# The MLP's up projection by one level of Strassen's recursion, in two passes of 1024 latent tokens, with the context tokens apart in native fp32

## The chip, the cores and the metric

The kernel runs on one core of one Trainium2 chip, in one launch. The metric is the device time in microseconds (us) of that core. The engines are TensorE (PE; its weight loads are listed as PEld), VectorE (DVE), ScalarE (ACT), GpSimd (POOL) and SyncE (SP), which issues most of the DMAs. All data is fp32; an fp32 number goes through TensorE either as native fp32 or, rounded, as fp32r.

## The reference, cut to what matters

One layer of a hybrid DeltaNet / Conformer backbone with a gated MLP, for 2048 latent tokens (a grid of 32 rows of 64) and 128 context tokens of width 1024. The change touches the first half of the MLP alone:

```python
h = rmsnorm(x, g_pre_ffn) * (1.0 + scale_f) + shift_f
gt, up = jnp.split(h @ w_up, 2, axis=-1)          # w_up: 1024 x 5632
gt = (dwconv2d_grid(gt, conv_ffn) if grid else dwconv1d(gt, conv_ffn[1])) + b_conv_ffn
y = (jax.nn.silu(gt) * up) @ w_down               # w_down: 2816 x 1024
x = x + gate_f * rmsnorm(y, g_post_ffn)
```

The depthwise convolution is 3x3 over the grid for latent tokens and 3 taps along the row for context tokens. `h` and `w_up` are split by both kernels into a high fp32r part and a low rest; a product is then three fp32r matmuls: high by high, high by low, low by high.

## The kernel before, in words

The stages follow each other: norm and input projection, short convolutions and the gated delta rule, output projection (lines up to 1173), MLP up (1177 to 1308), MLP down (1311 to 1366). Features lie on the partitions, tokens along the row. A scheduler orders each engine's instructions; every engine runs its own list in order and waits on semaphores.

The output projection handles 17 chunks of 128 tokens: the context chunk first, chunks 8 to 15, and chunks 0 to 7 last. After the matmuls of a chunk (line 1122), its norm runs on ACT and DVE (1131 to 1145), TensorE transposes it (1151) and ACT writes the normed, modulated chunk `ht` (1154). Chunks 0 to 7 are split at once into `h2H` and `h2L` in SBUF (1158, 1159); the others go to the DRAM tensor `d_h2` and are read back and split at lines 1207 to 1210.

MLP up has 44 weight tiles of 128 columns: 22 for the gate half, 22 for the up half. `load_up` (1190) brings one tile from DRAM, ACT writes its high part (1196), POOL the low rest (1197). `project_up` (1212) multiplies the tile with all 2176 tokens in blocks of 512, 512, 512, 320 and 320, each with 8 slices of the contraction times 3 matmuls (1220 to 1222). For a gate tile, `gate_in` copies the result into the padded grid `gb` on ACT (1245); `gate_conv` runs the 9 taps on DVE over all 2048 latent tokens (1256, then 8 times 1258), the context row beside it (1260, 1262), and silu on ACT (1263). For an up tile, `do_up` multiplies the PSUM block into `acc` on DVE (1269) and sends `acc` to the DRAM tensor `d_y`. The convolution of tile j runs beside the matmuls of up tile j-1 and of gate tile j+1.

MLP down reads `d_y` back by token chunk, splits it (1335 on ACT, 1336 on DVE), and multiplies with 22 weight tiles `wd`, each split by ACT (1323) and DVE (1324), in two halves of 512 output columns, 2244 matmuls in all (1339 to 1341). The weights of the first half are loaded and split while MLP up still runs.

## Time and profile before

| what | value |
|---|---|
| median of 3 runs | 2883.85 us (2879.0 to 2900.59) |
| span of the profiled execution, first to last instruction | 2883.5 us |
| MLP up on TensorE, first matmul to the first one of MLP down | 1309.07 to 2360.50, 1051.4 us |
| MLP down on TensorE, first matmul to the end of the span | 2360.50 to 2883.5, 523 us |
| DVE busy in the span | 1760.5 us, 61% |
| POOL busy in the span | 574.1 us, 20% |

The profiled execution is the span; nothing else is known to lie around it, and it agrees with the median to 0.4 us. The profile lists groups of instructions by source line with busy time, mean duration and the idle time before them; the timeline lists instructions with start and duration. A duration reaches from the start of an instruction to its end, and back-to-back instructions of one engine overlap a little, so the spacing of starts is what an instruction costs its engine.

### The profile page before, as it was taken

To read this page: it belongs to the slowest core of one execution; us is meant where nothing else is said; L and a number is where in the kernel's file an instruction comes from. 1 tells how busy PE (TensorE), PEld (TensorE's weight loads), DVE (VectorE), ACT (ScalarE), POOL (GpSimd) and SP (SyncE) were. 2 spreads that over 40 slices of the span, in tenths; PEclk is the share of its full clock that TensorE was granted. 3 is DMA by queue.
4 is the path that set the end of the run, shared out by engine and by line. 5 is a ranking of instruction groups with operands and counts; after the bars stand their busy time and mean duration, and the time that the engine had idled before them with its cause. 6 is when DMAs were issued, how large, how long until landed. Compare 5 with 4: busy or idle time off the path is not lost.

```text
span 2883.5 us, 40010 instructions
## 1 busy us (share of the span) xinstructions
PE 2769.5 (96%) x16077; PEld 2362.1 (82%) x16077; DVE 1760.5 (61%) x1929; ACT 962.6 (33%) x1992; POOL 574.1 (20%) x629
## 2 busy tenths in 40 slices
PE   7999999788899999999999999999999999999998
PEld 4888888677788887887888888888888888888887
DVE  4898999976667755564967454555555463224443
ACT  6432222445666656663111111111111122224221
POOL 2210011267165643222311111111111100000000
PEclk9999999899889999999999999999999999999999
DMA  7033522565886636643122111111111153336543
GB/s 266 20 90 115 149 83 70 113 188 132 228 261 182 188 111 242 195 137 125 49 72 83 38 54 38 54 38 53 38 54 38 50 169 111 98 97 203 173 164 119
DMA packets 341365, 337.77 MB, mean 117 GB/s; under 512 B 113990, under 2 KB 258620, under 8 KB 340924
## 3 DMA queue, kind: packets, MB, share of 16 engines
q1 hardware_dynamic: 329372, 321.59, 37.2%
q10 hardware_dynamic: 11808, 13.63, 1.4%
q8 instruction: 126, 2.06, 0.3%
q14 instruction: 59, 0.48, 0.1%
HBM read 240.35 MB, written 94.81 MB: 116 GB/s over the span
## 4 chain that ended last, share of the span: by engine, by line
PE 65%; DMA 5%; DVE 3%; POOL 3%; SPq 2%; ACT 2%; issue 2%; DVEq 0%; ACTq 0%; POOLq 0%
PE ps L1222 12%; PE ps L1220 12%; PE ps L1221 12%; PE ps L1122 6%; PE ps L1339 6%; PE ps L1341 6%; PE ps L1340 6%; SPq L164 1%; DMA ws<-in_wdown_dram 1%; DVE dm L817 1%; POOL bigB L150 1%; POOL prod L147 1%; PE p L955 1%; PE p L943 1%; PE p L925 1%
## 5 line engine op out<-in xcount | busy, mean ns | idle before, releaser
L1220 PE MATMUL ps<-h2H,wr 128*128 128x512 f32 (+1 forms) x1760 | 634.2, 360 | 3.1 <-DVE wr L1196 3.1
L1222 PE MATMUL ps<-h2H,wr 128*128 128x512 f32 (+1 forms) x1760 | 633.0, 360 | 1.7 <-POOL wr L1197 1.7
L1221 PE MATMUL ps<-h2L,wr 128*128 128x512 f32 (+1 forms) x1760 | 633.5, 360 | 0.0
L1258 DVE SCALAR_TENSOR_TENSOR acc<-gb,pvf,acc 128x2048 f32<-128x2048 f32 x176 | 419.5, 2388 | 1.3
L1220 PEld LDWEIGHTS ps<-h2H,wr 128*128 128x128 f32 x1760 | 330.7, 188 | 49.8 <-DVE wr L1196 3.4
L1222 PEld LDWEIGHTS ps<-h2H,wr 128*128 128x128 f32 x1760 | 330.8, 188 | 48.8 <-POOL wr L1197 2.1
L1221 PEld LDWEIGHTS ps<-h2L,wr 128*128 128x128 f32 x1760 | 330.8, 188 | 46.2
L359 PE MATMUL ps<-hH,wr 128*128 128x512 f32 (+1 forms) x960 | 349.7, 369 | 6.4 <-ACT bigA L410 4.1
L360 PE MATMUL ps<-hL,wr 128*128 128x512 f32 (+1 forms) x960 | 352.3, 367 | 0.0
L361 PE MATMUL ps<-hH,wr 128*128 128x512 f32 (+1 forms) x960 | 349.6, 365 | 0.0
L1197 POOL TENSOR_TENSOR wr<-wt,wr 128x1024 fp32r<-128x1024 f32 x44 | 128.9, 2930 | 882.7 <-ACT wr L1196 879.3
L1339 PE MATMUL ps<-wd,yr 128*128 128x512 f32 x748 | 291.9, 391 | 2.7 <-ACT wd L1323 2.6
L1340 PE MATMUL ps<-wd,yr 128*128 128x512 f32 x748 | 291.7, 390 | 0.0
L1341 PE MATMUL ps<-wd,yr 128*128 128x512 f32 x748 | 291.2, 390 | 0.0
L1256 DVE TENSOR_SCALAR acc<-gb,pvf 128x2048 f32<-128x2048 f32 x22 | 29.6, 1346 | 411.2 <-ACT gb L1245 405.7
L373 DVE SCALAR_TENSOR_TENSOR acc<-bigA,pvt,acc 128x1024 f32<-128x1024 f32 (+2 forms) x168 | 250.5, 1491 | 11.7 <-ACT acc L370 7.5
L359 PEld LDWEIGHTS ps<-hH,wr 128*128 128x128 f32 x960 | 183.8, 193 | 33.0 <-ACT bigA L410 4.6
L361 PEld LDWEIGHTS ps<-hH,wr 128*128 128x128 f32 x960 | 185.2, 193 | 25.1 <-issue 2.6
L360 PEld LDWEIGHTS ps<-hL,wr 128*128 128x128 f32 x960 | 185.5, 193 | 23.9 <-issue 1.6
L1336 DVE TENSOR_TENSOR yr<-yt,yr 128x1408 fp32r<-128x1408 f32 x68 | 110.6, 1626 | 150.5 <-ACT yr L1335 150.5
L1196 ACT CAST wr<-wt 128x1024 fp32r<-128x1024 f32 x43 | 45.4, 1056 | 446.0 <-issue 423.7
L1245 ACT COPY gb<-ps 128x512 f32<-128x512 f32 (+2 forms) x110 | 55.2, 503 | 362.2 <-PE ps L1222 349.9
...
## 6 DMA issues: line engine op xcount, KB each, us to landing
...
```

The costliest lines, as they stand in the source:

```text
L359: nc.tensor.matmul(ps[:, 0:n], wr[:, 0, k], hH[bi][:, k], start=(k == 0), stop=False)
L360: nc.tensor.matmul(ps[:, 0:n], wr[:, 0, k], hL[bi][:, k], start=False, stop=False)
L361: nc.tensor.matmul(ps[:, 0:n], wr[:, 1, k], hH[bi][:, k], start=False, stop=(k == KD - 1))
L373: nc.vector.scalar_tensor_tensor(dst, src[:, o + t:o + t + n], w[:, t:t + 1], dst, ALU.mult, ALU.add)
L1122: nc.tensor.matmul(pss[hf][:], a[:, k], w[k][:, 512 * hf:512 * hf + 512], start=(w is woH and a is mH and k == KD - 1), stop=(w is woL and ...
L1220: nc.tensor.matmul(ps[:, 0:n], wr[:, 0, k], h2H[bi][:, k], start=(k == 0), stop=False)
L1221: nc.tensor.matmul(ps[:, 0:n], wr[:, 0, k], h2L[bi][:, k], start=False, stop=False)
L1222: nc.tensor.matmul(ps[:, 0:n], wr[:, 1, k], h2H[bi][:, k], start=False, stop=(k == KD - 1))
L1258: nc.vector.scalar_tensor_tensor(al, gb[:, t // 3:t // 3 + 32, t % 3:t % 3 + 64], w[:, t:t + 1], al, ALU.mult, ALU.add)
L1339: nc.tensor.matmul(ps[:], yr[:, 0, i], wd[:, 0], start=(q == 0 and i == 0), stop=False)
L1340: nc.tensor.matmul(ps[:], yr[:, 0, i], wd[:, 1], start=False, stop=False)
L1341: nc.tensor.matmul(ps[:], yr[:, 1, i], wd[:, 0], start=False, stop=(q == 1 and i == HN - 1))
```

## The change

MLP up is rewritten. The context chunk is taken out: `ctx_unit` multiplies its 128 tokens with unsplit fp32 weights, 16 native fp32 matmuls of 128 columns for each of 22 units. The latent tokens are done in two passes p of 1024 tokens. In a pass the 1024 x 1024 block of `h` is cut in quarters (two halves of the contraction by two halves of the tokens), and a pair of weight tiles (gate tile j, up tile j) likewise. Strassen's recursion in Winograd's form makes 7 products of the 8: `build_T` forms the 7 token operands T0 to T6 once in a pass, `prep` the 7 weight operands for each unit (p, j), and `product` is 4 slices times 3 matmuls of 512 columns. So a unit has 84 matmuls of 512 columns; there are 44 units. `unit` adds the products up: in PSUM where two share a bank, else on DVE and POOL. `gate` runs the convolution for the 15 (p = 0) or 17 (p = 1) grid rows that a pass can finish; two rows and a strip of `up` go through the new DRAM tensor `d_hal` to the second pass.

All chunks of the output projection now go to `d_h2`; the SBUF copies of chunks 0 to 7 are gone. The first tap moves from DVE to ACT. The scheduler's order of every engine is unchanged up to the end of the output projection.

```diff
-            if c < 8:
-                o = slice(c % 4 * P, c % 4 * P + P)
-                nc.vector.tensor_copy(h2H[c // 4][:, :, o], ht[:])
-                nc.vector.tensor_tensor(h2L[c // 4][:, :, o], ht[:], h2H[c // 4][:, :, o].bitcast(F32), ALU.subtract)
-            else:
-                nc.scalar.dma_start(d_h2[:, :, c * P:(c + 1) * P], ht[:])
+            nc.scalar.dma_start(d_h2[:, :, c * P:(c + 1) * P], ht[:])
...
-        def project_up(m):
-            nonlocal npb
-            wr = first.pop() if first else load_up(m)
-            for bi in range(5):
-                s, n = BLOCKS[bi]
-                ps = (pmm if npb % 8 else pmx).tile([P, 512], F32, name="ps4", tag="mm")
-                npb += 1
-                for k in range(KD):
-                    nc.tensor.matmul(ps[:, 0:n], wr[:, 0, k], h2H[bi][:, k], start=(k == 0), stop=False)
-                    nc.tensor.matmul(ps[:, 0:n], wr[:, 0, k], h2L[bi][:, k], start=False, stop=False)
-                    nc.tensor.matmul(ps[:, 0:n], wr[:, 1, k], h2H[bi][:, k], start=False, stop=(k == KD - 1))
-                yield s, n, ps
...
+        hc = gp.tile([P, KD, P], F32, name="hc")
+        nc.sync.dma_start(hc[:], d_h2[:, :, CTX * P:NTOK])
...
+        T = [tp.tile([P, 2, HK, 512], F32R, name=f"T{i}") for i in range(7)]
...
+        def raw(src):
+            t = rp.tile([P, HK, P], F32, name="raw", tag="raw")
+            nc.sync.dma_start(t[:], src)
+            return t
+
+        def quarters(j):
+            return [raw(wup[m, :, HK * q:HK * q + HK, :]) for m in (j, NF + j) for q in range(2)]
...
+        def ctx_unit(j):
+            qs = quarters(j)
+            gpr = gprs[j % 2]
+            ps = pmm.tile([P, 2, P], F32, name="psc", tag="mm")
+            for g in range(2):
+                for k in range(KD):
+                    nc.tensor.matmul(ps[:, g], qs[2 * g + k // HK][:, k % HK], hc[:, k], start=(k == 0), stop=(k == KD - 1))
+            nc.scalar.copy(gpr[:, 1:129], ps[:, 0])
...
+        def split(dst, src, eng):
+            nc.scalar.copy(dst[0], src)
+            eng.tensor_tensor(dst[1], src, dst[0].bitcast(F32), ALU.subtract)
+
+        def build_T(p, k):
+            f = lambda t: t[:].rearrange("p a b -> p (a b)")
+            o = 1024 * p
+            b11, b21, b12, b22 = (raw(d_h2[:, kk, a:a + 512].rearrange("p (a b) -> p a b", b=P))
+                                  for a in (o, o + 512) for kk in (k, HK + k))
+            t1, t2, t4 = (sp.tile([P, HK, P], F32, name="ts", tag="s") for _ in range(3))
+            d = lambda i: (T[i][:, 0, k], T[i][:, 1, k])
+            split(d(0), f(b11), nc.gpsimd)
+            split(d(1), f(b21), nc.vector)
+            nc.vector.tensor_tensor(f(t1), f(b12), f(b11), ALU.subtract)
+            split(d(2), f(b22), nc.gpsimd)
+            nc.vector.tensor_tensor(f(t2), f(b22), f(t1), ALU.subtract)
+            split(d(4), f(t1), nc.vector)
+            nc.vector.tensor_tensor(f(b12), f(b22), f(b12), ALU.subtract)
+            split(d(5), f(t2), nc.vector)
+            nc.vector.tensor_tensor(f(t4), f(b21), f(t2), ALU.subtract)
+            split(d(6), f(b12), nc.gpsimd)
+            split(d(3), f(t4), nc.vector)
...
+        def prep(j):
+            a11, a12, a21, a22 = quarters(j)
+            s1, s2, s4_ = (sp.tile([P, HK, P], F32, name="ts", tag="s") for _ in range(3))
+
+            def combo(src):
+                wr = wp.tile([P, 2, HK, P], F32R, name="wr4", tag="wr")
+                split((wr[:, 0], wr[:, 1]), src[:], nc.gpsimd)
+                return wr
+
+            W = [None] * 7
+            with tc.high_priority():
+                nc.gpsimd.tensor_tensor(s1[:], a21[:], a22[:], ALU.add)
+                nc.gpsimd.tensor_tensor(s2[:], s1[:], a11[:], ALU.subtract)
+                nc.vector.tensor_tensor(a21[:], a11[:], a21[:], ALU.subtract)
+                W[0] = combo(a11)
+                W[5] = combo(s2)
+                nc.vector.tensor_tensor(s4_[:], a12[:], s2[:], ALU.subtract)
+                W[4] = combo(s1)
+                W[6] = combo(a21)
+                W[1] = combo(a12)
+                W[2] = combo(s4_)
+                W[3] = combo(a22)
+            return W
...
+        def product(ps, W, i, first):
+            for k in range(HK):
+                h, l = W[i][:, 0, k], W[i][:, 1, k]
+                nc.tensor.matmul(ps[:], h, T[i][:, 0, k], start=(first and k == 0), stop=False, skip_group_check=True)
+                nc.tensor.matmul(ps[:], h, T[i][:, 1, k], start=False, stop=False, skip_group_check=True)
+                nc.tensor.matmul(ps[:], l, T[i][:, 0, k], start=False, stop=(k == HK - 1), skip_group_check=True)
...
+            pa, x1 = bank(), xt()
+            product(pa, W, 0, True)
+            with tc.high_priority():
+                nc.scalar.copy(x1[:], pa[:])
+            pb, u2 = bank(), xt()
+            product(pb, W, 5, True)
+            with tc.high_priority():
+                nc.vector.tensor_tensor(u2[:], pb[:], x1[:], ALU.add)
+            pc, x5 = bank(), xt()
+            product(pc, W, 4, True)
+            with tc.high_priority():
+                nc.scalar.copy(x5[:], pc[:])
+            pd = bank()
+            product(pd, W, 6, True)
+            with tc.high_priority():
+                nc.vector.tensor_tensor(c22, pd[:], u2[:], ALU.add)
+                nc.gpsimd.tensor_tensor(c22, c22, x5[:], ALU.add)
+            product(pa, W, 1, False)
+            with tc.high_priority():
+                nc.scalar.copy(g1, rows(pa[:]))
+            product(pc, W, 2, False)
+            with tc.high_priority():
+                nc.vector.tensor_tensor(g2, rows(pc[:]), rows(u2[:]), ALU.add)
+            product(pd, W, 3, False)
+            with tc.high_priority():
+                nc.vector.tensor_tensor(c21, pd[:], u2[:], ALU.add)
...
+            nc.scalar.activation(al, gb[:, 0:nr, 0:64], AF.Identity, scale=w[:, 0:1], bias=bias)
             for t in range(1, 9):
+                nc.vector.scalar_tensor_tensor(al, gb[:, t // 3:t // 3 + nr, t % 3:t % 3 + 64], w[:, t:t + 1], al,
...
+            nc.scalar.activation(acc[:, 0:n], acc[:, 0:n], AF.Silu)
+            nc.vector.tensor_tensor(acc[:, 0:n], acc[:, 0:n], up[:, 0:n], ALU.mult)
...
+        for p in range(2):
+            for i in range(HALF):
+                if i in (1, 3, 5, 7):
+                    build_T(p, i // 2)
+                ctx_unit(HALF * p + i)
+            W = prep(0)
+            prev = None
+            for j in range(NF):
+                up = ep.tile([P, 1088], F32, name="up4", tag="up")
+                if p == 1:
+                    nc.sync.dma_start(gbs[j % 2][:, 0:2, 1:65], d_hal[j, :, 0:2])
+                    nc.sync.dma_start(up[:, 0:64], d_hal[j, :, 2])
+                Wn = prep(j + 1) if j < NF - 1 else None
+                unit(p, j, W, up)
+                if p == 0 and j > 1:
                     next(mg, None)
-            if j == 0:
-                gens = [gate_in(0), gate_in(1)]
-                for _ in range(len(BLOCKS)):
-                    for g in gens:
-                        next(g)
-                for g in gens:
-                    run(g)
-            elif j > 1:
-                run(gate_in(j))
-            acc = gate_conv(j)
-            if prev is not None:
-                do_up(j - 1, prev)
-            prev = acc
-            if j == 8:
-                put_gate(1, "gpostf", 40, big, ("gm", 1), pmm, "mm")
-        do_up(NF - 1, prev)
-
-    # ------------------------------------------------------------------ gated MLP, down
-    sR.close()
+                    next(mg, None)
+                gate(p, j, up)
+                W = Wn
```

On DVE, in the steady state of MLP up, before: one gate tile's convolution (`acc`, from the grid `gb` and the taps `pvf`), with the first two of the five PSUM multiplications of the preceding up tile (1269) between its taps.

```order
L1256 TENSOR_SCALAR acc_15375<-gb_12723,pvf 128x2048
L1260 TENSOR_SCALAR acc_15375<-gpr_12725,pvf 128x128
L1258 SCALAR_TENSOR_TENSOR acc_15375<-gb_12723,pvf,acc_15375 128x2048
L1262 SCALAR_TENSOR_TENSOR acc_15375<-gpr_12725,pvf,acc_15375 128x128
L1258 SCALAR_TENSOR_TENSOR acc_15375<-gb_12723,pvf,acc_15375 128x2048
L1262 SCALAR_TENSOR_TENSOR acc_15375<-gpr_12725,pvf,acc_15375 128x128
L1269 TENSOR_TENSOR acc_15082<-acc_15082,ps_15394 128x512
L1258 SCALAR_TENSOR_TENSOR acc_15375<-gb_12723,pvf,acc_15375 128x2048 x2
L1269 TENSOR_TENSOR acc_15082<-acc_15082,ps_15420 128x512
```

Now, at the same place (pass 0, some unit j): the whole cycle of one unit.

```order
L1260 TENSOR_TENSOR ts<-raw,ts 128x512
L1324 SCALAR_TENSOR_TENSOR acc_15592<-gb_12684,pvf,acc_15592 128x960
L1313 TENSOR_TENSOR up_15456<-ps_15538,x_15509 128x512
L1324 SCALAR_TENSOR_TENSOR acc_15592<-gb_12684,pvf,acc_15592 128x960 x3
L1295 TENSOR_TENSOR x_15661<-ps_15660,x_15646 128x512
L1324 SCALAR_TENSOR_TENSOR acc_15592<-gb_12684,pvf,acc_15592 128x960 x2
L1257 TENSOR_TENSOR raw<-raw 128x512
L1324 SCALAR_TENSOR_TENSOR acc_15592<-gb_12684,pvf,acc_15592 128x960
L1303 TENSOR_TENSOR up_15608<-ps_15690,x_15661 128x512
L1324 SCALAR_TENSOR_TENSOR acc_15592<-gb_12684,pvf,acc_15592 128x960
L1330 TENSOR_TENSOR acc_15592<-acc_15592,up_15456 128x960
L1310 TENSOR_TENSOR gb_12685<-ps_15675,x_15661 128x8x64
```

A unit now has on DVE 8 taps of 960 (p = 1: 1088) elements, the product with `up` (1330) and two weight sums (1257, 1260), all with both tensors in SBUF, and four additions with one tensor in PSUM (1313, 1295, 1303, 1310). Line 1303, which the seventh product of the unit waits for, stands behind seven of the eight taps.

On POOL the stage had one row before, line 1197, the low rest of a weight tile of 1024, 44 times in all. Now one unit has ten rows of 512: seven low rests (1223), two weight sums (1255, 1256) and one addition to `up` (1304).

```order
L1304 TENSOR_TENSOR up_15456<-up_15456,x_15524 128x512
L1223 TENSOR_TENSOR wr_15484<-raw,wr_15484 128x512
L1223 TENSOR_TENSOR wr_15487<-ts,wr_15487 128x512
L1223 TENSOR_TENSOR wr_15490<-raw,wr_15490 128x512
L1223 TENSOR_TENSOR wr_15623<-raw,wr_15623 128x512
L1223 TENSOR_TENSOR wr_15626<-ts,wr_15626 128x512
L1255 TENSOR_TENSOR ts<-raw 128x512
L1223 TENSOR_TENSOR wr_15630<-ts,wr_15630 128x512
L1256 TENSOR_TENSOR ts<-ts,raw 128x512
L1223 TENSOR_TENSOR wr_15633<-raw,wr_15633 128x512
```

POOL writes each weight operand a unit ahead of its use; line 1304 waits for DVE's line 1303 of the same unit, and DVE's lines 1257 and 1260 wait for POOL's 1255 and 1256.

On DVE at the end of MLP up, the last convolution now has the splits of the down weights (`wd`, 1388) between its taps, thirteen of them ahead of the product with `up` (1330) and eight more behind it, and only then the first split of `yr` (1400):

```order
L1324 SCALAR_TENSOR_TENSOR acc_20445<-gb_12685,pvf,acc_20445 128x1088
L1388 TENSOR_TENSOR wd_20541<-ws_20539,wd_20541 128x512
L1388 TENSOR_TENSOR wd_20546<-ws_20544,wd_20546 128x512
L1388 TENSOR_TENSOR wd_20551<-ws_20549,wd_20551 128x512
L1330 TENSOR_TENSOR acc_20445<-acc_20445,up_20343 128x1088
L1388 TENSOR_TENSOR wd_20556<-ws_20554,wd_20556 128x512
```

Before, these splits stood between the PSUM multiplications of the last up tile, whose convolution was long done:

```order
L1324 TENSOR_TENSOR wd_19128<-ws_19126,wd_19128 128x512
L1269 TENSOR_TENSOR acc_18807<-acc_18807,ps_18962 128x512
L1324 TENSOR_TENSOR wd_19133<-ws_19131,wd_19133 128x512
L1269 TENSOR_TENSOR acc_18807<-acc_18807,ps_18989 128x512
L1324 TENSOR_TENSOR wd_19138<-ws_19136,wd_19138 128x512
```

What moved: the convolution of the last unit and the weight splits of MLP down now stand behind the last matmul of MLP up, ahead of the first matmul of MLP down, whose operand `yr` lies in the SBUF space of the last `acc`.

## Rows read from the trace of the kernel before

**Rows 1.** The page's busy times: engine, us, share of the span, instructions.

```profile
PE 2769.5 (96%) x16077; PEld 2362.1 (82%) x16077; DVE 1760.5 (61%) x1929; ACT 962.6 (33%) x1992; POOL 574.1 (20%) x629
```

**Rows 2.** Windows: us, then busy us (instructions) of each engine, PEclk, DMA share, GB/s.

```profile
2.00:40.00 38.00, 24.60 (x104) 9.56 (x105) 8.91 (x18) 15.81 (x23) 7.57 (x4) 0.96 1.01 372
...
1358.00:2357.00 999.00, 999.00 (x5077) 866.38 (x5076) 585.63 (x415) 148.21 (x198) 123.75 (x42) 1.00 0.18 54
```

**Rows 3.** Timeline of PE: 48 matmuls of 320 columns begin, then 24 of 512.

```profile
2329.78 0.30 PE L1220 MATMUL ps<-h2H,wr 128*128 128x320 f32 x1
...
2336.81 0.40 PE L1220 MATMUL ps<-h2H,wr 128*128 128x512 f32 x1
...
2342.40 0.39 PE L1220 MATMUL ps<-h2H,wr 128*128 128x512 f32 x1
```

**Rows 4.** Timeline of POOL and of DVE, 1386 to 1408 us.

```profile
1386.79 16.62 POOL L1197 TENSOR_TENSOR wr<-wt,wr 128x1024 fp32r<-128x1024 f32 x1 [19.78 <-ACT wr L1196]
...
1394.27 11.28 DVE L1258 SCALAR_TENSOR_TENSOR acc<-gb,pvf,acc 128x2048 f32<-128x2048 f32 x4
```

**Rows 5.** Timeline of DVE: spacing of taps of 2048 and of 128.

```profile
1460.66 2.34 DVE L1258 SCALAR_TENSOR_TENSOR acc<-gb,pvf,acc 128x2048 f32<-128x2048 f32 x1
1462.92 0.34 DVE L1262 SCALAR_TENSOR_TENSOR acc<-gpr,pvf,acc 128x128 f32<-128x128 f32 x1
1463.18 2.34 DVE L1258 SCALAR_TENSOR_TENSOR acc<-gb,pvf,acc 128x2048 f32<-128x2048 f32 x1
```

**Rows 6.** Timeline of POOL and of DVE about 1434 us and 1722 us.

```profile
1434.17 2.87 POOL L1197 TENSOR_TENSOR wr<-wt,wr 128x1024 fp32r<-128x1024 f32 x1 [21.13 <-ACT wr L1196]
...
1434.70 4.50 DVE L1258 SCALAR_TENSOR_TENSOR acc<-gb,pvf,acc 128x2048 f32<-128x2048 f32 x1
...
1722.05 2.53 POOL L1197 TENSOR_TENSOR wr<-wt,wr 128x1024 fp32r<-128x1024 f32 x1 [20.91 <-ACT wr L1196]
...
1722.21 0.48 DVE L1269 TENSOR_TENSOR acc<-acc,ps 128x320 f32<-128x320 f32 x1
```

**Rows 7.** Timeline of PE: native fp32 matmuls of 128 columns, 8 of the program's.

```profile
867.77 1.95 PE L955 MATMUL p<-y,pt 128*128 128x128 f32 x16
```

**Rows 8.** Groups by form: line, engine, tiles, shape | busy us, mean ns | idle before, releaser.

```profile
L1258 DVE SCALAR_TENSOR_TENSOR acc<-gb,pvf,acc 128x2048 f32<-128x2048 f32 x176 | 419.5, 2388 | 1.3
L1197 POOL TENSOR_TENSOR wr<-wt,wr 128x1024 fp32r<-128x1024 f32 x44 | 128.9, 2930 | 882.7 <-ACT wr L1196 879.3 <-DVE wr L1196 3.4
L1324 DVE TENSOR_TENSOR wd<-ws,wd 128x512 fp32r<-128x512 f32 x44 | 28.8, 690 | 22.7 <-ACT wd L1323 22.7
L1358 DVE TENSOR_TENSOR ot<-ot,xt 128x1024 f32<-128x1024 f32 x17 | 20.8, 1225 | 0.6
L319 POOL TENSOR_TENSOR hL<-st,hH 128x512 fp32r<-128x512 f32 x12 | 16.2, 1350 | 38.2 <-DVE hH L317 36.6 <-DVE isk L297 1.6
L1100 POOL TENSOR_TENSOR on<-on,sc 128x512 f32<-128x512 f32 x17 | 17.7, 1041 | 34.2 <-DVE sc L1099 17.0 <-ACT junk L1126 11.2 <-DVE rs L1133 4.1
L1323 ACT CAST wd<-ws 128x512 fp32r<-128x512 f32 x44 | 26.7, 620 | 30.3 <-DMA ws<-in_wdown_dram 29.7
```

**Rows 9.** Line 964 alone, POOL, 128x512: duration ns min/median/max.

```profile
L964 POOL TENSOR_TENSOR on<-on x17: 1262/1592/2870, 816.0 to 1090.4; 128x512 f32<-128x512 f32 x17
```

**Rows 10.** The chain of waits: a load of 256 KB.

```profile
886.70 3.79 DMA qt<-d_kq
```

**Rows 11.** Timeline at the start of MLP up: ACT, then PE.

```profile
1319.79 2.90 ACT L1154 ACTIVATE ht<-pt,modT,scg 128x128 f32<-128x128 f32 x8
...
1309.07 0.50 PE L1220 MATMUL ps<-h2H,wr 128*128 128x512 f32 x1 [3.12 <-DVE wr L1196]
...
1311.50 0.80 PE L1222 MATMUL ps<-h2H,wr 128*128 128x512 f32 x1 [1.70 <-POOL wr L1197]
```

**Rows 12.** The chain of waits, PE's steps just after that wait.

```profile
1316.14 0.43 PE ps L1220
...
1317.59 0.23 PE ps L1222
```

More of the change, by code (lines that the diff above doesn't have):

```diff
@@ L1225, in hybrid_step_kernel @@
[L1225 to L1232 removed]
+        rp = s4.enter_context(tc.tile_pool(name="rp4", bufs=8, reuse_waits="tile"))
+        wp = s4.enter_context(tc.tile_pool(name="wp4", bufs=7, reuse_waits="tile"))
+        sp = s4.enter_context(tc.tile_pool(name="sp4", bufs=3, reuse_waits="tile"))
@@ new lines, in hybrid_step_kernel, with taps @@
+        gbs = [gp.tile([P, 19, 66], F32, name=f"gb{i}") for i in range(2)]
+        gprs = [gp.tile([P, 130], F32, name=f"gpr{i}") for i in range(2)]
+        for t in gbs + gprs:
+            nc.gpsimd.memset(t[:], 0.0)
+        def raw(src):
[4 more added lines that the diff above has]
+            return [raw(wup[m, :, HK * q:HK * q + HK, :]) for m in (j, NF + j) for q in range(2)]
+        def taps(j):
+            return pvf[:, 9 * j:9 * j + 9], pvf[:, 198 + j:199 + j]
@@ new lines, in ctx_unit @@
+        def ctx_unit(j):
[6 more added lines that the diff above has]
+            nc.scalar.copy(gpr[:, 1:129], ps[:, 0])
+            w, bias = taps(j)
+            ac = ep.tile([P, P], F32, name="acx", tag="acx")
+            nc.scalar.activation(ac[:], gpr[:, 0:128], AF.Identity, scale=w[:, 3:4], bias=bias)
+            for t in range(1, 3):
+                nc.vector.scalar_tensor_tensor(ac[:], gpr[:, t:t + 128], w[:, 3 + t:4 + t], ac[:], ALU.mult, ALU.add)
+            nc.scalar.activation(ac[:], ac[:], AF.Silu)
+            nc.vector.tensor_tensor(ac[:], ac[:], ps[:, 1], ALU.mult)
+            nc.sync.dma_start(d_y[CTX, :, j, :], ac[:])
```

123 lines of the change are left out of this document (41 added, 82 removed).

## The prediction

> **What bounds the kernel now.** I read the page's busy times first: TensorE is busy 96% of the span, DVE 61%, POOL 20% [rows 1]. Taken over the whole program that says that fewer columns through TensorE save time and that POOL has room. The windows say more: from 1358 to 2357 us, MLP up, TensorE never rests (999 of 999 us, clock 1.00), DVE works 586 us and POOL 124 us [rows 2]. So the stage lasts as long as its matmuls do. Their price is the spacing of starts on the timeline: 48 matmuls of 320 columns take 7.03 us, 0.147 us each, and 24 of 512 take 5.59 us, 0.233 us each [rows 3]. Check: 3168 matmuls of 512 and 2112 of 320 make 738 + 310 = 1048 us; the stage took 1051.4 us.
>
> The third view is the timeline of POOL and DVE side by side, for what happens when both want to work. A POOL low rest (line 1197) that met an unbroken chain of DVE taps took 16.62 us, and the four taps among which it came through took 11.28 us instead of four times 2.26 [rows 4, 5]. Where POOL came first, the next tap took 4.50 us instead of 2.34 [rows 6]. But beside line 1269, which reads one tensor from PSUM, POOL's 2.53 us and DVE's 0.48 us ran at the same time at no loss [rows 6]. So a DVE instruction with both tensors in SBUF and a POOL instruction exclude each other. Before, this costs nothing: POOL has one row per weight tile.
>
> **TensorE's part of the change.** A unit is 84 matmuls of 512 columns, 84 x 0.233 = 19.6 us; 44 units make 862 us, 186 us less than 1048. The context units add 352 native fp32 matmuls of 128 columns. The trace has 16 records in 1.95 us for 8 such matmuls, 0.24 us each [rows 7], so 3.9 us a unit and 86 us in all. TensorE alone would gain 100 us.
>
> **DVE and POOL in a unit.** Taps: 2048 elements cost 2.26 us and 128 cost 0.26 us from start to start [rows 5], so 1.04 ns an element over a base of 0.13 us; 960 elements cost 1.13 us and 1088 cost 1.26 us. Eight of them are 9.0 us in pass 0 and 10.1 us in pass 1. The product with `up` reads two SBUF tensors: from 1225 ns for 1024 elements [rows 8], 1.1 and 1.25 us. The two weight sums, like line 1324 at 690 ns less an overlap of 0.08 us [rows 5, 8], are 1.2 us. That is 11.3 us (12.55 us in pass 1) in which DVE shuts POOL out. POOL's ten rows are 128x512 with two tensors: line 319 does just that in 1.35 us on average beside a busy DVE [rows 8], line 964 in 1.262 us at its quickest [rows 9], and line 1100, whose second tensor is narrower, in 1.04 us [rows 8]. I take 1.27 us, the undisturbed price of the same form; the ends are 1.04 and 1.54 us (half of line 1197's mean of 2930 is 1.47 us, line 964's mean lies above). Ten cost 12.7 us.
>
> The two exclude each other, so a unit costs 11.3 + 12.7 = 24.0 us in pass 0 and 25.25 us in pass 1, against TensorE's 19.6 us. DVE's four additions from PSUM run beside POOL rows and add nothing. I followed the order of one unit to see whether the turn is ever unused: POOL gets in at each of the four PSUM additions, while DVE waits for ACT's silu, and where lines 1257 and 1260 wait for POOL; that carries all ten rows, so I add no waste. With POOL at 1.04 us a unit is 22 us, with 1.47 us 26 us. TensorE will rest some 4 to 5 us in each unit, mostly ahead of the seventh product, which waits for DVE's line 1303 behind seven taps. ACT has seven 512-casts of 0.62 us [rows 8], 4.3 us; even at a microsecond each its five other rows leave it under 10 us, and it binds nothing.
>
> The Trainium skill has this rule (page "SBUF — State Buffer", section "Who interferes with whom"): a VectorE instruction with two SBUF inputs and a GpSimd instruction that reads SBUF use one shared port, and the later one is blocked until the earlier one has finished. The trace agrees on the single instruction but goes further: in 16.62 us POOL was passed over by several taps, not one. By the rule POOL would have every second turn; by the row it must wait for a break in DVE's chain. The sum of the two is 24.0 us either way.
>
> **Lead-in, change of pass, end.** Before the first product of a pass, 60 loads of 256 KB (11 units x 4, and 16 for the T operands) and the T sums must be done. At the best rate seen, 372 GB/s [rows 2], 15.7 MB take 42 us. But there are eight `raw` buffers, so two groups of four take turns: a chain of two T groups, five context units and the first weight load. A load takes 3.79 us [rows 10], a context unit 3.9 us, a T group 8 DVE rows of 0.61 and 3 POOL rows of 1.27 us, 8.7 us: 2 x 12.5 + 5 x 7.7 + 3.8 = 67 us. Buffers come free one by one, so I take 60 us. In pass 0 the chain starts when the last chunk of `h` has reached DRAM. Its `ht` was written at 1319.8 to 1322.7 us [rows 11]; without the POOL and DVE rows of the old start it comes a little earlier, so about 1321 with its store. The first product follows at about 1382, 73 us after the old first matmul at 1309.07 [rows 11]. Nothing hides these 73 us but the 43 us of context matmuls in them. At the change of pass the loads begin in the last unit, when its first product frees T0: some 14 us ahead, 46 us left, and the last convolution competes with the T sums, so 50 us (bounds 30 and 75).
>
> At the end DVE still has seven taps (8.8 us), the product (1.25 us), 21 weight splits at 0.61 us (12.8 us) and two waits for ACT of about 1 us before MLP down can begin: 25 us with TensorE at rest, where before there was no gap. Bounds: 12 us, if the splits come earlier, and 35 us, if the loads of the weights hold them up. MLP down itself is unchanged.
>
> **The sum.** Lead-in 73; pass 0 19.6 + 21 x 24.0 = 523.6 (in the first unit no convolution runs yet); change of pass 50; pass 1 19.6 + 20 x 25.25 + 20 = 544.6 (in the last no weights are prepared); end 25. Together 1216 us where 1051.4 stood: 165 us more. The span of the profiled execution is 2883.5 us, 0.4 us below the median, so about 3050 us.
>
> **Rivals.**
> 1. *TensorE stays the bound* (DVE and POOL fit beside each other). For it: 19.6 us is more than either engine's own 14 or 13 us. Against it: rows 4 and 6. Time: 73 + 862 + 50 + 25 = 1010, 41 us less, 2842 us, faster by 1.4%. It decides as soon as the two lists exclude each other for less than 19.6 us a unit; with the gaps in between at 30 and 50 us it is 2799 us.
> 2. *The turns are badly shared.* POOL is passed over as in rows 4, weights come late, DVE waits for TensorE, and some 3 to 4 us of each unit go unused: 28 and 29 us a unit, 42 x 3.9 = 163 us more, about 3210 us. Against it: no unbroken chain in the new order is longer than three taps.
> 3. *TensorE falls to its low clock.* After waits of 3.12 and 1.70 us its matmuls were spaced 0.43 us until 1316.1 and 0.23 us from 1317.6 on [rows 11, 12], the lower and the upper of its two levels. With a wait in each unit a stretch like that, five us at half rate, costs 2.5 us; 19.6 + 2.5 is still below 24.0 us, and nothing changes. If it stayed low for good, a unit would take 84 x 0.43 = 36 us, and the whole 690 us more, 3570 us. The Trainium skill (page "TensorE: Matmul & The Clock Gate", section "HAM oscillation — how this bites in real kernels") tells of kernels that fall back to the low clock at every wait; the trace shows such a fall, but with full speed again after five us.
>
> **How the numbers follow.** Forecast 0.80, rival 1 0.06, rival 2 0.11, rival 3 0.03. The likeliest's own range comes from POOL's price (22 to 26 us a unit, -84 to +84 us) and the bounds of the gaps, 2960 to 3150. Rival 1 lies outside below; of rival 2 I take in the nearer part: 2965 to 3185. About 1% can be told from no change here. Faster by over 1% is most of rival 1: 0.05; within 1%: 0.03; slower: 0.92.
>
> **What would show it.** Right: in the passes POOL and DVE together are busy or blocked nearly all the time, taps and POOL rows show means well above 1.13 and 1.27 us because they wait inside, a unit takes 24 to 25 us, TensorE rests 4 to 5 us in each, released by DVE's line 1303 or POOL's 1223; and it rests some 30, 20 and 25 us at the lead-in, the change of pass and the end. Wrong: units of 19.6 us with TensorE unbroken (rival 1), POOL rows of many us with TensorE waiting on 1223 alone (rival 2), matmuls spaced 0.43 us all through (rival 3), or gaps outside their bounds.

## The result, and the profile after

The changed kernel takes 3037.25 us (median of 4 runs, 3030.53 to 3046.91) against 2882.66 us before: ratio 1.0532, 95% interval 1.0495 to 1.0569. The forecast was 3050 us. The profiled execution has a span of 3028.7 us, 145.2 us more than before.

The page's busy times of the changed kernel, which answer to [rows 1]:

```profile
PE 2719.5 (90%) x15309; PEld 2267.9 (75%) x15309; DVE 2141.8 (71%) x2290; ACT 1206.4 (40%) x2441; POOL 1303.9 (43%) x1049
```

TensorE's busy time fell by 50 us and the kernel is 145 us slower: DVE's busy time grew by 381 us and POOL's by 730 us. For POOL that is more than the new rows cost at undisturbed prices: 440 rows of the units at 1.27 us are 559 us. The windows answer to [rows 2] (us, busy us and instructions of PE, PEld, DVE, ACT and POOL, then PEclk, DMA share, GB/s); the first two are stretches of some twenty units in pass 0 and in pass 1, the others the end, the lead-in and the change of pass.

```profile
1395.00:1870.00 475.00, 423.13 (x1847) 338.19 (x1846) 412.20 (x303) 157.73 (x247) 355.67 (x204) 0.94 0.27 79
1960.00:2440.00 480.00, 414.88 (x1670) 334.26 (x1669) 436.56 (x295) 157.02 (x240) 416.74 (x204) 0.92 0.24 69
...
2470.00:2506.00 36.00, 0.46 (x3) 0.13 (x1) 27.24 (x34) 16.44 (x24) 0.00 (x0) 0.55 0.78 264
1309.00:1372.00 63.00, 47.48 (x353) 46.13 (x353) 39.00 (x62) 30.40 (x68) 17.69 (x13) 0.89 0.82 268
1886.00:1945.00 59.00, 49.02 (x357) 46.79 (x356) 46.11 (x67) 24.80 (x53) 17.45 (x11) 0.88 0.84 266
```

In pass 1 DVE is "busy" 437 and POOL 417 of 480 us, though their rows at undisturbed prices are some 15 and 13 us of a 24 us unit. The rest is waiting that the records count as busy, as the groups of that stretch show, and behind them TensorE's line of the stretch in pass 0 (line, engine, tiles, shapes | busy us, mean ns | idle before, releaser):

```profile
L1324 DVE SCALAR_TENSOR_TENSOR acc<-gb,pvf,acc 128x1088 f32<-128x1088 f32 x156 | 301.7, 1934 | 6.1 <-ACT acc L1322 1.7
L1271 PE MATMUL ps<-T,wr 128*128 128x512 f32 x556 | 231.1, 416 | 65.1 <-DVE up L1303 65.1
...
L1223 POOL TENSOR_TENSOR wr<-ts,wr 128x512 fp32r<-128x512 f32 x61 | 139.9, 2295 | 0.0
...
L1257 DVE TENSOR_TENSOR raw<-raw 128x512 f32<-128x512 f32 x20 | 34.3, 1715 | 0.6 <-POOL ts L1255 0.6
...
L1303 DVE TENSOR_TENSOR up<-ps,x 128x512 f32<-128x512 f32 x20 | 13.6, 678 | 2.1 <-PE ps L1273 2.1
```

```profile
L1271 PE MATMUL ps<-T,wr 128*128 128x512 f32 x567 | 234.0, 413 | 51.0 <-DVE up L1303 51.0
```

Lines 1257 and 1303 show the case best. Both are additions (or subtractions) of 128x512 on DVE. Line 1303 reads one tensor from PSUM and takes 0.68 us on average; line 1257 reads both from SBUF and takes 1.72 us. TensorE's idle time ahead of these products has one releaser, line 1303: 65.1 us in 19 waits in the stretch of pass 1, 51.0 us in that of pass 0. The prediction had named it. On the timeline one sees the turns. DVE (the three taps together, then the last two of them one by one), then POOL (start, duration):

```profile
2096.29 6.39 DVE L1324 SCALAR_TENSOR_TENSOR acc<-gb,pvf,acc 128x1088 f32<-128x1088 f32 x3
2102.60 0.68 DVE L1295 TENSOR_TENSOR x<-ps,x 128x512 f32<-128x512 f32 x1
...
2098.11 2.27 DVE L1324 SCALAR_TENSOR_TENSOR acc<-gb,pvf,acc 128x1088 f32<-128x1088 f32 x1
...
2100.41 2.27 DVE L1324 SCALAR_TENSOR_TENSOR acc<-gb,pvf,acc 128x1088 f32<-128x1088 f32 x1
```

```profile
2094.97 4.26 POOL L1223 TENSOR_TENSOR wr<-raw,wr 128x512 fp32r<-128x512 f32 x2 [1.41 <-ACT wr L1222]
2099.19 2.34 POOL L1223 TENSOR_TENSOR wr<-ts,wr 128x512 fp32r<-128x512 f32 x1
2101.61 2.23 POOL L1255 TENSOR_TENSOR ts<-raw 128x512 f32<-128x512 f32 x1
```

Three taps take 6.39 us instead of 3.8, and between them POOL's rows take up to 2.34 us each instead of 1.27: one tap, one POOL row, one tap. The first of the three follows an addition from PSUM, beside which POOL had begun its row, and takes 1.78 us; where taps and POOL rows alternate without a break, the taps start 2.30 us apart (2098.11 and 2100.41). Line 1295, from PSUM, takes its 0.68 us in the middle of a POOL row.

The terms of the sum, measured by the starts of the first and last matmuls of each stretch on the timeline:

| term | forecast, us | measured, us |
|---|---|---|
| old start 1309.07 to the first product (1372.06) | 73 | 63.0 |
| pass 0, a unit (mean of 21) | 24.0 | 23.5 |
| pass 0 and change of pass, to 1945.35 | 573.6 | 573.3 |
| pass 1, a unit (mean of 21) | 25.25 | 24.1 |
| pass 1 | 544.6 | 524.8 |
| last product to first matmul of MLP down (2505.88) | 25 | 35.7 |
| MLP up in all | 1216 | 1196.8 |

MLP down took 522.8 us, as before. The first row leans on two executions: the output projection's last matmul ended at 1299.1 us in this one and at 1305.1 us in that of the kernel before, though its order is unchanged. How the lead-in begins, ACT's write of the last `ht`, and its store in the chain of waits:

```profile
1308.60 2.90 ACT L1150 ACTIVATE ht<-pt,modT,scg 128x128 f32<-128x128 f32 x8 [2.32 <-PE pt L1147]
...
1311.54 3.49 DMA d_h<-ht
```

### The profile page after: what moved, and what is told of

Same layout as the page of the kernel before. It is cut to its first block, busy times and chain, and to the rows that moved or that the text cites. A ratio compares the mean times of both kernels' runs of the same rounds, so it can differ in the third digit from the quotient of the medians.

```text
span 3028.7 us, 41386 instructions
## 1 busy us (share of the span) xinstructions
PE 2719.5 (90%) x15309; PEld 2267.9 (75%) x15309; DVE 2141.8 (71%) x2290; ACT 1206.4 (40%) x2441; POOL 1303.9 (43%) x1049
## 4 chain that ended last, share of the span: by engine, by line
PE 32%; DVE 21%; issue 11%; DMA 8%; ACT 5%; POOL 4%; SPq 2%; POOLq 0%; DVEq 0%; ACTq 0%
DVE acc L1324 12%; PE ps L1118 6%; PE ps L1405 5%; PE ps L1403 5%; PE ps L1404 5%; POOL wr L1223 2%; DVE raw L1257 1%; DMA raw<-in_wup_dram 1%; PE ps L1271 1%; DVE dm L818 1%; PE ps L1272 1%; PE ps L1273 1%; DMA ws<-in_wdown_dram 1%; ACT acc L1322 1%; ACT acc L1329 1%
## 5 line engine op out<-in xcount | busy, mean ns | idle before, releaser
L1324 DVE SCALAR_TENSOR_TENSOR acc<-gb,pvf,acc 128x960 f32<-128x960 f32 (+1 forms) x352 | 630.6, 1791 | 14.4 <-ACT acc L1322 7.2
L1271 PE MATMUL ps<-T,wr 128*128 128x512 f32 x1232 | 509.6, 414 | 123.3 <-DVE up L1303 118.5
L1272 PE MATMUL ps<-T,wr 128*128 128x512 f32 x1232 | 501.9, 407 | 0.0
L1273 PE MATMUL ps<-T,wr 128*128 128x512 f32 x1232 | 499.9, 407 | 0.6 <-POOL wr L1223 0.6
L1271 PEld LDWEIGHTS ps<-T,wr 128*128 128x128 f32 x1232 | 244.9, 199 | 194.2 <-DVE up L1303 135.5
L1223 POOL TENSOR_TENSOR wr<-raw,wr 128x512 fp32r<-128x512 f32 x176 | 313.1, 1786 | 71.6 <-ACT wr L1222 70.0
L1403 PE MATMUL ps<-wd,yr 128*128 128x512 f32 x748 | 292.8, 392 | 36.3 <-ACT yr L1399 35.5
L1273 PEld LDWEIGHTS ps<-T,wr 128*128 128x128 f32 x1232 | 244.1, 198 | 55.4 <-POOL wr L1223 1.3
L1272 PEld LDWEIGHTS ps<-T,wr 128*128 128x128 f32 x1232 | 246.4, 200 | 51.4
L1223 POOL TENSOR_TENSOR wr<-ts,wr 128x512 fp32r<-128x512 f32 x132 | 258.0, 1956 | 16.8 <-ACT wr L1222 16.5
L361 PEld LDWEIGHTS ps<-hL,wr 128*128 128x128 f32 x960 | 183.4, 191 | 24.1 <-issue 1.6
L280 POOL TENSOR_TENSOR wr<-wt,wr 128x1024 fp32r<-128x1024 f32 x24 | 68.8, 2866 | 285.0 <-ACT wr L279 284.5
L1403 PEld LDWEIGHTS ps<-wd,yr 128*128 128x128 f32 x748 | 140.9, 188 | 67.5 <-ACT yr L1399 36.5
```

The source lines that it names most:

```text
L361: nc.tensor.matmul(ps[:, 0:n], wr[:, 0, k], hL[bi][:, k], start=False, stop=False)
L1223: eng.tensor_tensor(dst[1], src, dst[0].bitcast(F32), ALU.subtract)
L1271: nc.tensor.matmul(ps[:], h, T[i][:, 0, k], start=(first and k == 0), stop=False, skip_group_check=True)
L1272: nc.tensor.matmul(ps[:], h, T[i][:, 1, k], start=False, stop=False, skip_group_check=True)
L1273: nc.tensor.matmul(ps[:], l, T[i][:, 0, k], start=False, stop=(k == HK - 1), skip_group_check=True)
L1324: nc.vector.scalar_tensor_tensor(al, gb[:, t // 3:t // 3 + nr, t % 3:t % 3 + 64], w[:, t:t + 1], al, ALU.mult, ALU.add)
```

## The experiments

All runs start from the changed kernel; "a unit" is the mean of 21 units, from the first product of the first to that of the last unit of a pass, pass 0 / pass 1. The changed kernel has 23.5 / 24.1 us. Experiments 1 to 9 have one execution each. In the profiles the output projection's last matmul ends between 1295.3 us (experiment 6) and 1310.7 us (experiment 10), so spans differ by up to 15 us for that alone; units and gaps do not depend on it.

**1. Two taps fewer.**

```diff
-            for t in range(1, 9):
+            for t in range(1, 7):
```

> The last two of the eight DVE taps (line 1324) are left out, so the convolution is incomplete; all else stays. The changed kernel's profile has 23.5 us a unit in pass 0 and 24.1 us in pass 1, span 3028.7 us. Theory (a DVE instruction with two SBUF tensors and a POOL instruction exclude each other, so a unit is the sum of both lists): a unit loses two taps of 1.13 / 1.26 us, 21.3 us in pass 0 and 21.6 us in pass 1, span about 3029 - 21 x 2.26 - 20 x 2.52 = 2931 us. Rival 'POOL's own list is the bound' (ten rows that take 1.7 to 2.3 us each whatever DVE does): units as before, span within 10 us of 3029. Rival 'DVE's own list is the bound': also minus 2.3 to 2.5 us a unit; it is told apart by the run without two POOL rows.

Measured: 22.0 / 22.0 us a unit, span 2942.9 us. 86 us less; 78 of them in the passes, and 10 at the end, where the last convolution is shorter (26.0 us). POOL's own list is not the bound. The sum without two taps is 21.7 / 22.7 us.

**2. Two POOL rows fewer.**

```diff
+                if not low:
+                    nc.scalar.copy(wr[:, 0], src[:])
+                    return wr
...
-                W[1] = combo(a12)
-                W[2] = combo(s4_)
+                W[1] = combo(a12, False)
+                W[2] = combo(s4_, False)
```

> Two of the seven low rests on POOL (line 1223, operands W1 and W2) are left out; their products take the high part twice, with as many matmuls, so the output lacks these low rests. Theory (the lists of DVE and POOL add up): a unit loses two POOL rows of 1.27 us, 21.0 us in pass 0 and 21.6 us in pass 1, span about 3029 - 43 x 2.54 = 2920 us. Rival 'POOL's own list is the bound': the rows' durations in the trace, 1.7 to 2.3 us, count in full, minus 3.4 to 4.5 us, so TensorE's 19.6 us decides, span about 2860 us. Rival 'DVE's own list is the bound': units of 23.5 and 24.1 us as before, span within 10 us of 3029.

Measured: 22.1 / 23.0 us, span 2980.4 us. 48 us less: DVE's list alone is not the bound either, but the two rows were worth 1.5 and 1.1 us a unit, not 2.5. Against the sum itself the units stand well (11.3 + 8 x 1.27 = 21.5, and 22.7 us): the changed kernel had come out 0.5 and 1.2 us under its sum, this one 0.6 and 0.3 us over it. The records show where the gain went: the time in which neither a DVE row with two SBUF tensors nor a POOL row runs grew from 0.9 / 0.6 us a unit in the changed kernel to 1.7 / 1.8 us here.

**3. The seven low rests on DVE.**

```diff
-                split((wr[:, 0], wr[:, 1]), src[:], nc.gpsimd)
+                split((wr[:, 0], wr[:, 1]), src[:], nc.vector)
```

> All seven low rests of a unit (line 1223) go from POOL to DVE; POOL keeps three rows. Theory (the lists add up): seven rows at 0.61 instead of 1.27 us, the sum falls by 4.6 us to 19.4 us (pass 0) and 20.65 us (pass 1); DVE's own list is then 11.3 + 4.3 + 2.4 = 18 us and 19.3 us plus a wait of about 1.2 us for silu. I expect 20 us a unit in pass 0 and 21 us in pass 1, span about 3029 - 21 x 3.5 - 21 x 3.1 = 2890 us. Rival 'DVE's own list is the bound': 4.3 us more a unit, 28 us, span about 3210 us. Rival 'POOL's own list is the bound': POOL is nearly empty, units of 19.6 us, span about 2855 us.

Measured: 21.1 / 20.9 us, span 2931.3 us. DVE gets 4.3 us a unit more to do and the kernel is 97 us faster, which of the three theories only the exclusion explains. Pass 0 is 1.1 us above the expectation and 1.7 us above the sum of 19.4. For 2.1 us a unit (1395 to 1800 us) neither a DVE row with two SBUF tensors nor a POOL row runs: with three POOL rows left, DVE's four additions from PSUM find few of them to run beside, and DVE as a whole is busy 394.6 of these 405 us. In a stretch of pass 0 the taps now take 1.34 us on average, near their 1.20:

```profile
L1324 DVE SCALAR_TENSOR_TENSOR acc<-gb,pvf,acc 128x960 f32<-128x960 f32 x152 | 203.4, 1338 | 1.2 <-ACT acc L1322 0.7
...
L1257 DVE TENSOR_TENSOR raw<-raw 128x512 f32<-128x512 f32 x19 | 27.6, 1454 | 3.0 <-POOL ts L1255 1.8 <-DMA raw<-in_wup_dram 1.2
```

Line 1257, which stands beside one of POOL's three remaining rows, still shows 1.45 us.

**4. No POOL row at all.** As 3, and also:

```diff
-                nc.gpsimd.tensor_tensor(s1[:], a21[:], a22[:], ALU.add)
-                nc.gpsimd.tensor_tensor(s2[:], s1[:], a11[:], ALU.subtract)
+                nc.vector.tensor_tensor(s1[:], a21[:], a22[:], ALU.add)
+                nc.vector.tensor_tensor(s2[:], s1[:], a11[:], ALU.subtract)
...
-                nc.scalar.copy(x5[:], pc[:])
+                nc.vector.tensor_tensor(x5[:], pc[:], u2[:], ALU.add)
...
-                nc.vector.tensor_tensor(c22, pd[:], u2[:], ALU.add)
-                nc.gpsimd.tensor_tensor(c22, c22, x5[:], ALU.add)
+                nc.vector.tensor_tensor(c22, pd[:], x5[:], ALU.add)
```

> POOL gets no row of MLP up's units at all: its seven low rests and two weight sums go to DVE, and its addition of x5 is replaced by one DVE addition out of PSUM (line 1299 becomes pc + u2 on DVE, so line 1303 alone finishes c22). Theory (DVE's and POOL's rows exclude each other): with nobody to wait for, every tap takes its undisturbed 1.20 us (960 elements) or 1.34 us (1088), lines 1257 and 1260 0.68 us, in place of means of 1.74, 1.93, 1.6 and 1.1 us. A unit is DVE's own list: taps 9.0, product 1.1, eleven rows of 0.61 and five additions from PSUM of 0.61, 19.9 us in pass 0 and 21.1 us in pass 1, with a wait for silu of up to 1.2 us on top: 20.4 and 21.5 us, span about 3029 - 21 x 3.1 - 21 x 2.6 = 2909 us. Rival 'the rows are long for another reason (DMA or TensorE reading the same SBUF)': the taps stay at means above 1.5 us; DVE's list is then over 25 us and the span over 3050 us.

Measured: 19.6 / 20.5 us, span 2888.1 us, 141 us less with one engine doing the work of two. Its groups in a stretch of pass 0:

```profile
L1323 DVE SCALAR_TENSOR_TENSOR acc<-gb,pvf,acc 128x960 f32<-128x960 f32 x155 | 187.7, 1224 | 0.9 <-ACT acc L1321 0.9
...
L1299 DVE TENSOR_TENSOR x<-ps,x 128x512 f32<-128x512 f32 x20 | 13.6, 682 | 0.0
...
L1257 DVE TENSOR_TENSOR raw<-raw 128x512 f32<-128x512 f32 x19 | 13.0, 684 | 0.0
```

Taps 1.22 us, and line 1257 takes 0.684 us, the same as the PSUM additions. DMA and TensorE read the same memory as before, so they do not lengthen DVE's rows; POOL did. In pass 0 TensorE has no rest left (busy 383.6 of the 385 us from 1395 to 1780), so 19.6 us is its pace as well as DVE's; in pass 1 DVE's list is the unit (busy 392.5 of the 400 us from 1890 to 2290).

**5. POOL rows that read one tensor.**

```diff
-                split((wr[:, 0], wr[:, 1]), src[:], nc.gpsimd)
+                nc.scalar.copy(wr[:, 0], src[:])
+                nc.gpsimd.tensor_copy(wr[:, 1], src[:])
```

> On POOL the seven low rests (line 1223, two SBUF tensors read) become copies of the weight sums (one SBUF tensor read), so the low rests are wrong and the work of a unit keeps its number of rows. The run asks whether a POOL row that reads one tensor excludes DVE's taps as well. If it does, the copies and the taps show means well above their shortest duration, as in the changed kernel (POOL 1.79 and 1.96 us against 1.27; taps 1.71 and 1.88 us against 1.20 and 1.34), and a unit is DVE's 11.3 / 12.55 us plus 3 x 1.27 us plus seven times the copy's own price, which no row of POOL shows so far: with 1.27 us 23.5 us a unit as before, span 3029 us; with 0.65 us 19.8 / 21 us, span about 2900 us. If it does not, the copies always take their shortest duration, taps grow only beside the three rows with two tensors, units fall to TensorE's 19.0 to 19.9 us and the span to about 2860 us.

Measured: 19.9 / 20.5 us, span 2888.6 us. POOL's groups in a stretch of pass 0:

```profile
L1251 POOL CAST wr<-raw 128x512 fp32r<-128x512 f32 x82 | 88.2, 1081 | 36.0 <-PE ps L1274 23.9 <-issue 10.3 <-DVE acc L1325 1.0
...
L1257 POOL TENSOR_TENSOR ts<-ts,raw 128x512 f32<-128x512 f32 x21 | 40.2, 1914 | 0.6
```

A copy that met no DVE row with two SBUF tensors takes 0.60 to 0.62 us (58 of them on the timelines of both passes); the 238 that met one have a median of 1.23 us; the first line's 82 copies have a mean of 1.08 us. So a row that reads one tensor excludes the taps too, but is done in half the time. With 0.61 us the sum is 11.3 + 3.8 + 4.3 = 19.4 and 20.65 us, against 19.9 and 20.5; of these only pass 1 tests the sum, since TensorE is busy 404.1 of the 405 us from 1395 to 1800 and sets the pace of pass 0 itself. The Trainium skill (page "SBUF — State Buffer", section "Who interferes with whom") has it so: any GpSimd instruction that reads SBUF contends with a VectorE instruction with two SBUF inputs. The trace agrees for both kinds of POOL row.

**6. Weight operands kept.** Stored in pass 0, loaded in pass 1.

```diff
+            if p == 1:
+                W = [None] * 7
+                for i in (0, 5, 4, 6, 1, 2, 3):
+                    W[i] = wp.tile([P, 2, HK, P], F32R, name="wr4", tag="wr")
+                    nc.sync.dma_start(W[i][:].bitcast(F32), d_w[j, i])
+                return W
...
+            for i in (0, 5, 4, 6, 1, 2, 3):
+                nc.sync.dma_start(d_w[j, i], W[i][:].bitcast(F32))
```

> The seven weight operands of a unit are stored to DRAM in pass 0 (3.7 MB a unit) and loaded in pass 1 instead of being formed again; the work of a unit of pass 0 stays. Theory (the lists add up): in pass 1 DVE has 10.1 + 1.25 us with two SBUF tensors and POOL one row, 12.6 us together, so TensorE decides: 19.6 us a unit, pass 1 is 94 us shorter. Pass 0 stays at 23.5 us; span about 2935 us. Rival 'the units of pass 1 are late for another reason' (the two extra loads of d_hal, the 17 rows, the store of acc): they stay at 24 us. Rival 'DMA becomes the bound': 3.7 MB more in each unit are 157 to 187 GB/s over the 70 to 80 GB/s of now; the stretch around the change of pass moved 266 GB/s at a busy share of 0.84; if that is the limit, units of pass 0 and 1 grow by what TensorE waits for loads (ACT waiting for raw in pass 0, TensorE for the loaded operand in pass 1).

Measured: 23.5 / 19.2 us, span 2913.5 us. Windows of pass 0 and pass 1:

```profile
1395.00:1800.00 405.00, 360.16 (x1578) 286.94 (x1577) 354.53 (x259) 132.73 (x209) 299.19 (x173) 0.94 0.69 236
1970.00:2340.00 370.00, 370.00 (x1634) 306.49 (x1633) 279.73 (x252) 79.97 (x98) 45.56 (x20) 1.00 0.71 228
```

With one POOL row a unit TensorE never rests in pass 1. The stores raise the traffic of pass 0 from 79 to 236 GB/s and its units stay at 23.5 us.

**7. The end: eight buffers for the loads of the down weights** (`bufs=8` for `ws5`).

> The change with eight instead of four buffers (ws) for the down weights' loads; nothing else. In the changed kernel's trace TensorE rests 35.9 us between the passes and MLP down, where I had worked out 25 us from DVE's list, with 35 us if the weights' loads hold up. If the loads through four buffers are what holds it up (ACT's casts wait for DMA between nearly all weights, 1.45 us a weight), eight buffers bring the gap to 26 to 30 us. If DVE's list and the place of yr behind the weight splits are the cause, the gap stays within 2 us of 36.

Measured: 32.6 us, span 3028.7 us. ACT's waits for the weights' loads in the gap fell from 16.3 to 7.9 us, but that the three us are the buffers' is not shown: in experiments 2 to 6 and 9, which leave the buffers alone, the gap lies between 30.7 and 36.3 us too. The span did not change. So the loads are not what holds up the most of it. In the trace `yt` is issued only at 2498.95, behind the store of the last `acc` at 2494.77.

**8. The end: another order of pools.**

```diff
-        rp = s4.enter_context(tc.tile_pool(name="rp4", bufs=8, reuse_waits="tile"))
+        ep = s4.enter_context(tc.tile_pool(name="ep4", bufs=2, reuse_waits="tile"))
...
-        ep = s4.enter_context(tc.tile_pool(name="ep4", bufs=2, reuse_waits="tile"))
+        rp = s4.enter_context(tc.tile_pool(name="rp4", bufs=8, reuse_waits="tile"))
```

> Only the order in which MLP up's SBUF pools are opened is changed (results, weight operands, weight sums, raw tiles, instead of raw tiles, weight operands, weight sums, results), so that the buffers yt and yr of MLP down come to lie on raw tiles and weight sums, which the last unit no longer uses, in place of the last acc. Theory from the run with eight ws buffers (gap 32.8 us, three less): the gap is the chain last convolution, store of acc, load of yt into its space, split of yr. Without it TensorE starts as soon as the first weight and yr are there, and then runs at the pace of the weights' loads, 1.45 us each for 0.7 us of matmuls: first matmul of MLP down 8 to 14 us after the last product instead of 35.9 us, of which half is lost again between the weights: span about 3029 - 12 = 3017 us. Rival (loads and DVE's weight splits bound it in any order): the first matmul comes earlier, but MLP down ends as late as before, span 3029 within 6 us.

Measured: TensorE starts after 12.4 us, but the span is 3025.9 us, 2.8 us less. Timeline of TensorE there (in brackets the wait and its releaser):

```profile
2473.94 0.39 PE L1273 MATMUL ps<-T,wr 128*128 128x512 f32 x1
2486.55 0.80 PE L1403 MATMUL ps<-wd,yr 128*128 128x512 f32 x1 [12.22 <-ACT yr L1399]
...
2495.31 0.79 PE L1403 MATMUL ps<-wd,yr 128*128 128x512 f32 x1 [5.02 <-ACT wd L1387]
2496.80 0.80 PE L1404 MATMUL ps<-wd,yr 128*128 128x512 f32 x1 [0.70 <-DVE wd L1388]
...
2500.79 0.79 PE L1403 MATMUL ps<-wd,yr 128*128 128x512 f32 x1 [2.77 <-ACT wd L1387]
```

Started earlier, TensorE waits for the weights one by one, and at the lower clock (granted 0.62 from 2474.3 to 2510 us); from the last product to the end of the span it takes 552 us instead of 559, about half of what was expected and little below the 554 to 560 us of experiments 2 to 6 and 9. What is late now is the weights, but not by their loads alone. On ACT the next cast of a weight waits for the store of the last `acc`:

```profile
2500.12 2.18 ACT L1387 CAST wd<-ws 128x512 fp32r<-128x512 f32 x4 [4.86 <-DMA d_y<-acc]
```

From 2474 to 2510 us ACT waits 8.1 us for loads of weights, 4.9 us for this store and 5.4 us for the last taps, behind which its silu and then the casts stand.

**9. Kept operands, and the low rests on DVE** (6 and 3 together, `x5` as in 4; POOL keeps lines 1255 and 1256).

> keep_w (weight operands stored in pass 0, loaded in pass 1) and lows_dve (the seven low rests on DVE) in one, and POOL's addition of x5 replaced by a DVE addition out of PSUM, so POOL keeps two rows, the weight sums of lines 1255 and 1256. Theory (the lists add up): pass 0 is DVE's 11.3 + 4.3 and POOL's 2.5 us, 18.1 us, DVE's own list 18.6 us, with the waste that lows_dve showed (21.1 us against a sum of 19.4) 20.3 us a unit; pass 1 is bound by TensorE at the 19.0 us of keep_w. From lows_dve's 2931 us: 21 x 0.8 and 21 x 1.9 us less, 2875 us. If the stores of pass 0 (3.7 MB a unit) lengthen units that no longer have time to spare, pass 0 stays at 21.1 us or more, and the span lies above 2890 us.

Measured: 20.1 / 19.2 us, span 2862.1 us, 2863.98 us beside 2895.18 us of the kernel before on the same chip.

**10. All of it: 4, 6, 7 and 8.**

> All in one: POOL without rows (no_pool), weight operands stored in pass 0 and loaded in pass 1 (keep_w), the order of pools of the run pools, and eight ws buffers. By the parts: lead-in 66 us, pass 0 at no_pool's 19.6 us a unit, 432 us, change of pass about 60 us, pass 1 at keep_w's 19.0 us, 418 us, end 36 - 15 us: 997 us against 1051 us of the kernel before, 2830 us. If the stores (3.7 MB a unit) lengthen the units of pass 0, which have no time to spare on DVE, to keep_lows_dve's 20.1 us, 2841 us; if the order of the end brings nothing, 2845 to 2855 us.

Measured: 2840.46 us (median of 4) against 2888.98 us of the kernel before on that chip, ratio 0.9824 (0.9796 to 0.9853). Its passes:

```profile
1395.00:1800.00 405.00, 403.10 (x1878) 329.12 (x1877) 387.80 (x498) 148.54 (x226) 1.63 (x1) 1.00 0.82 284
1970.00:2280.00 310.00, 310.00 (x1369) 256.76 (x1369) 243.03 (x228) 57.50 (x66) 0.00 (x0) 1.00 0.74 229
```

A unit takes 19.7 / 19.2 us, the DVE list in pass 0 not lengthened by the stores; TensorE rests 1.9 of 405 us in pass 0 and not at all in pass 1. With DMA at 284 GB/s the taps still take 1.21 us, which settles that DMA does not lengthen them:

```profile
L1332 DVE SCALAR_TENSOR_TENSOR acc<-gb,pvf,acc 128x960 f32<-128x960 f32 x151 | 180.9, 1212 | 0.1
```

From the last product to the end of the span it takes 544.6 us, 14 us less than in the changed kernel and well below the 554 us and more of the runs that leave the end alone. Eight buffers and the other order of pools bring this only together; what the emptied POOL adds to it was not separated.

From the first product to the first matmul of MLP down it is 924 us (1383.8 to 2308.0) against 1134 us in the changed kernel. Its first product came 11.7 us later, since the unchanged stages ahead of MLP up ended that much later in this execution. So Strassen's saving on TensorE is real; in the changed kernel it was paid back with interest on DVE and POOL.

## Why the prediction was right, step by step

- **DVE and POOL exclude each other, so a unit is the sum of two lists.** Shown by experiments 1 to 5: less of either list shortens the unit, and work taken from POOL and given to DVE shortens it most. The sum comes within 1.2 us of the unit in the changed kernel and in experiments 1 (21.7 / 22.7 us), 2 and 5; in experiment 3 it is 1.7 us short in pass 0.
- **POOL's price of 1.27 us.** Right: the shortest row 1223 in the passes is 1.27 us. 1.04 us would have given 21.7 and 22.95 us.
- **Pass 1 at 25.25 us, 544.6 in all.** 20 us too much, the largest error. A tap and a POOL row in unbroken alternation take 2.30 us, not 1.26 + 1.27 = 2.53: the exclusion is not quite as long as the two undisturbed durations. Against that stands waste, which the text put at nothing: for 0.9 us of a unit in pass 0 and 0.6 us in pass 1 neither a DVE row with two SBUF tensors nor a POOL row runs. The two errors partly cancel, and that the 24.0 us for pass 0 came within 0.5 us is in part luck. By the pair a POOL row is worth 2.30 - 1.26 = 1.04 us, so experiment 2 could bring about 2.1 us a unit; waste grew by 0.8 and 1.2 us there, which leaves about the 1.5 and 1.1 us measured. That is read from the records, not tested.
- **TensorE's part, 19.6 us a unit.** Too high: where nothing holds it up, a unit takes 19.0 us (84 matmuls). It changed nothing, since it was not the bound. The context matmuls took 92.7 us, not 86, at a granted clock of 0.88 to 0.89. The waits measured 51.0 / 20 = 2.6 us a unit in pass 0 and 65.1 / 20 = 3.3 us in pass 1, not 4 to 5; most of the remainder (1.3 of 1.9 us in pass 0, 1.8 us in pass 1) goes to matmuls spaced 0.42 us, at the lower clock, after the waits (granted 0.94 and 0.92), the mild form of rival 3, and is hidden under DVE and POOL, as the text said.
- **Lead-in 73 us.** Measured 63, and six of the ten us are not the forecast's: in this execution the output projection ended 5.9 us earlier than in that of the kernel before, from which the 73 us were counted. From its last matmul to the last `ht` it is 9.5 us, 14.7 before, about the five us that the text allowed for the rows of the old start. From the landing of that store (1315.0) to the first product it is 57 us against 61. Not all loads wait for that chunk (the first T loads were issued from 1308.15 us, the context matmuls began at 1309.2 us). From 1309 to 1372 us the chain of waits goes through loads of `raw` (30%), context matmuls (24%), stores of context rows (14%) and T rows in turn, which is the text's picture of buffers taking turns; with DMA busy 82% at 268 GB/s the loads alone are not excluded, and neither was tried by itself.
- **Change of pass 50 us.** 55.9 measured, within the bounds; it too runs at 266 GB/s and 84%. That pass 0 and this change together agree to 0.3 us is luck: pass 0 was 6 us shorter than forecast and the change 6 us longer.
- **End 25 us.** 35.7, just outside the bounds of 12 to 35 (30.7 to 36.3 in the runs that leave the end alone). DVE's list was sized about rightly (27.2 us busy in the gap), but two things named only as a bound came together: ACT waits for the weights' DMA 13 times in these 36 us, 16.3 us in all, and `yt` takes over the space of the last `acc`. Experiment 8 takes `yt` off that space, but a weight operand now waits for the same store, so it does not part the two causes; experiment 10, with both remedies, ends 14 us sooner.
- **The sum.** 1216 us against 1196.8: lead-in and pass 1 came out 30 us too long, the end 10.7 us too short.
- **The rivals.** Rival 1 (TensorE stays the bound) fell, and it is what experiment 10 makes true by emptying POOL and, in pass 1, by loading the operands. Rival 2 (28 to 29 us a unit) did not appear: single units of pass 0 reach some 28 us, the mean does not. Rival 3 as a permanent low clock did not appear.
